# Cross-entropy of 8192 rows: a masked sum instead of gathers, a fixed order with shrinking last loads, and a strip of 16 small DMAs

## The chip, the cores and the metric

One core of one Trainium2 chip. The metric is device time in microseconds (us), lower is better; a verdict needs 2%. All runs told here were in the fast state at a granted clock of 1.0. Runs of one kernel agree within about 0.9 us, and the kernel before, run again beside the others in four sets of rounds, has medians of 2440.05 to 2440.22 us; so I read differences of 1 us here, although they are only 0.04% of the time. The 95% intervals are about ±0.14% or 3.4 us: by them alone, differences under about 3 us are not clear. The profile's span is about 1.7 us shorter than the time.

## The reference

```python
logits = np.random.randn(16, 512, 32000).astype(np.float32)      # 1048.6 MB
labels = np.random.randint(0, 32000, (16, 512)).astype(np.int32)

logits_max = np.max(logits, axis=-1, keepdims=True)
log_sum_exp = np.log(np.sum(np.exp(logits - logits_max), axis=-1)) + logits_max.squeeze(-1)
loss = -(logits - log_sum_exp[..., np.newaxis])[rows, cols, labels]
```

The 8192 rows lie as 64 groups of 128 rows, one row in each partition. Each logit is read once. The kernels leave the maximum out, as these inputs allow.

## The kernel before

Two buffers of 128x16000 take turns; ScalarE does Exp in place with a row sum. The last three groups come in loads of 4000 columns. The label's logit of each row is fetched by one indirect DMA per group ("gather" below) out of the logits in memory.

```python
    for g in range(G):                          # 64 gathers of 128 elements
        nc.gpsimd.indirect_dma_start(out=lab_logit[:, g:g + 1], ..., in_=lg,
            in_offset=bass.IndirectOffsetOnAxis(ap=idx[:, g:g + 1], axis=1))
    ...
            for c in range(C):                  # C = 2 halves of 16000 columns
                t = data_pool.tile([P, W], FP32)            # bufs=2
                nc.sync.dma_start(out=t[:], in_=lg_pg[:, g, c * W:(c + 1) * W])
                nc.scalar.activation(out=t[:], in_=t[:], func=Exp,
                                     accum_out=stats_col(g, c))
    ...                                         # last 3 groups: the same with 4000 columns, bufs=5
    finalize(0, G - 1)                          # sum, Ln, subtract, store
    finalize(G - 1, G)
```

The softmax here doesn't subtract the row's maximum and nothing guards it: scores larger than these inputs give would overflow.

Of the kernel before, what the change touches and what calls it, by code (L numbers as in the profile page):

```python
# [1 line left out]

# [4 lines left out]

FP32 = mybir.dt.float32
I32 = mybir.dt.int32  # L10


@with_exitstack
def kernel(
    ctx: ExitStack,
    tc: tile.TileContext,
    logits: bass.AP,
    labels: bass.AP,
    out: bass.AP,
):  # L20
    nc = tc.nc

    B, S, V = logits.shape
    N = B * S
    P = 128
    G = N // P
    assert N % P == 0

    W = 16000
    C = V // W  # L30
    assert V % W == 0

    WF = 4000
    CF = V // WF
    FINE_GROUPS = 3
    assert V % WF == 0

    lg = logits.rearrange("b s v -> (b s) v")
    lg_pg = lg.rearrange("(p g) v -> p g v", g=G)
    labels_pg = labels.rearrange("b s -> (b s)").rearrange("(p g) -> p g", g=G)  # L40
    out_pg = out.rearrange("b s -> (b s)").rearrange("(p g) -> p g", g=G)

    data_pool = ctx.enter_context(tc.tile_pool(name="data", bufs=2))
    fine_pool = ctx.enter_context(tc.tile_pool(name="fine", bufs=5))
    persist = ctx.enter_context(tc.tile_pool(name="persist", bufs=1))

    labs64 = persist.tile([P, G], mybir.dt.int64)
    nc.sync.dma_start(out=labs64[:], in_=labels_pg)  # L48

    idx = persist.tile([P, G], I32)  # L50
    nc.gpsimd.iota(idx[:], pattern=[[V, G]], base=0, channel_multiplier=G * V)  # L51
    labs32 = labs64[:].bitcast(I32).rearrange("p (g two) -> p g two", two=2)[:, :, 0]
    nc.gpsimd.tensor_tensor(out=idx[:], in0=idx[:], in1=labs32, op=mybir.AluOpType.add)  # L53

    lab_logit = persist.tile([P, G], FP32)
    for g in range(G):
        nc.gpsimd.indirect_dma_start(  # L57
            out=lab_logit[:, g:g + 1],
            out_offset=None,
            in_=lg,  # L60
            in_offset=bass.IndirectOffsetOnAxis(ap=idx[:, g:g + 1], axis=1),
        )

    stats = persist.tile([P, G - 1, CF], FP32)
    stats_last = persist.tile([P, 1, CF], FP32)
    nc.vector.memset(stats[:], 0.0)  # L66

    def stats_col(g, c):
        return stats[:, g, c:c + 1] if g < G - 1 else stats_last[:, 0, c:c + 1]

    for g in range(G):
        if g >= G - FINE_GROUPS:
            for c in range(CF):
                tf = fine_pool.tile([P, WF], FP32)
                nc.sync.dma_start(out=tf[:], in_=lg_pg[:, g, c * WF:(c + 1) * WF])
                nc.scalar.activation(  # L76
                    out=tf[:], in_=tf[:],
                    func=mybir.ActivationFunctionType.Exp,
                    accum_out=stats_col(g, c),
                )  # L80
        else:
            for c in range(C):
                t = data_pool.tile([P, W], FP32)
                nc.sync.dma_start(out=t[:], in_=lg_pg[:, g, c * W:(c + 1) * W])  # L84
                nc.scalar.activation(  # L85
                    out=t[:], in_=t[:],
                    func=mybir.ActivationFunctionType.Exp,
                    accum_out=stats_col(g, c),
                )

    totals = persist.tile([P, G], FP32)
    logsum = persist.tile([P, G], FP32)
    res = persist.tile([P, G], FP32)

    def finalize(lo, hi):
        nc.vector.reduce_sum(  # L96
            out=totals[:, lo:hi],
            in_=stats[:, lo:hi, :] if hi <= G - 1 else stats_last[:],
            axis=mybir.AxisListType.X,
        )  # L100
        nc.scalar.activation(  # L101
            out=logsum[:, lo:hi], in_=totals[:, lo:hi],
            func=mybir.ActivationFunctionType.Ln,
        )
        nc.vector.tensor_tensor(  # L105
            out=res[:, lo:hi], in0=logsum[:, lo:hi], in1=lab_logit[:, lo:hi],
            op=mybir.AluOpType.subtract,
        )
        nc.scalar.dma_start(out=out_pg[:, lo:hi], in_=res[:, lo:hi])  # L109

    finalize(0, G - 1)
    finalize(G - 1, G)


# [1 line left out]
_INS = ['logits', 'labels']  # L116
_OUTS = [((16, 512), 'float32')]


# [23 lines left out]
```

## Time and profile before

| | before |
|---|---|
| time, median | 2440.22 us (2440.01 to 2440.32) |
| read from memory | 1048.67 MB, 430 GB/s over the span |
| ScalarE / VectorE busy | 72% / 0% |
| steady distance of big loads | 18.90 us (8.192 MB, so 433 GB/s) |
| from the last landing to the end of the span | 7.9 us |

ScalarE waits for every big load (642.9 us idle), so the loads set the pace. The timeline of ScalarE in the middle (start, duration, what, idle before and cause):

```profile
349.45 13.54 ACT L85 ACTIVATE t<-t 128x16000 f32<-128x16000 f32 x1 [5.28 <-DMA t<-in_logits_dram]
...
368.35 13.54 ACT L85 ACTIVATE t<-t 128x16000 f32<-128x16000 f32 x1 [5.26 <-DMA t<-in_logits_dram]
...
387.25 13.54 ACT L85 ACTIVATE t<-t 128x16000 f32<-128x16000 f32 x1 [5.28 <-DMA t<-in_logits_dram]
```

An activation that waited for its load starts about 0.5 us after the last row of that load has ended (0.54 us in the median of the 122 big loads, from the packets of this trace), so these starts are a clock of landings: one every 18.90 us. The same timeline at the end:

```profile
2430.84 3.54 ACT L76 ACTIVATE tf<-tf 128x4000 f32<-128x4000 f32 x1 [1.11 <-DMA tf<-in_logits_dram]
...
2434.49 1.28 ACT L101 ACT_TABLE_LOAD   x1
...
2435.78 0.20 ACT L101 ACTIVATE logsum<-totals 128x1 f32<-128x1 f32 x1
2436.02 0.16 DVE L105 TENSOR_TENSOR res<-logsum,lab_logit 128x1 f32<-128x1 f32 x1 [1.35 <-ACT logsum L101]
```

The last tile landed at 2430.8; Exp, a table load, Ln, the subtraction and the store follow, 7.9 us in all.

### The profile page before, as it was taken

What the parts mean: (1) busy time and instruction counts of PE and PEld (TensorE: products, weight loads), DVE (VectorE), ACT (ScalarE), POOL (GpSimd) and SP (SyncE); (2) the same over time, 40 slices, a digit from 0 to 9 for tenths busy, and PEclk for the clock granted to TensorE, in tenths of its full rate; (3) what the DMA queues carried; (4) which work ended last, traced back from release to release, by engine and by line L of the source; (5) the groups of instructions that cost most, each with busy time, mean ns of one, the idle gap of its engine ahead of it and who ended that gap; (6) DMA issues with size and microseconds to landing.
All of it is one profiled execution on the core that took longest, in us unless ns stands there. A gap on an engine that the chain in (4) does not pass through costs nothing.

```text
span 2438.7 us, 851 instructions
## 1 busy us (share of the span) xinstructions
DVE 1.7 (0%) x5; ACT 1754.4 (72%) x298; POOL 61.2 (3%) x70
## 2 busy tenths in 40 slices
DVE  0000000000000000000000000000000000000000
ACT  4777766777677767777677767777677767777697
POOL 3222000000000000000000000000000000000000
DMA  9999999999999999999999999999999999999998
GB/s 404 437 420 422 435 437 435 429 429 437 437 436 428 431 435 437 435 432 428 435 436 436 435 427 434 436 437 435 427 432 436 437 435 425 434 437 432 426 430 360
DMA packets 23510, 1048.77 MB, mean 430 GB/s; under 512 B 4688, under 2 KB 4816, under 8 KB 4816
## 3 DMA queue, kind: packets, MB, share of 16 engines
q1 hardware_dynamic: 21168, 1048.65, 99.6%
q0 software_dynamic: 2048, 0.04, 0.1%
q10 hardware_dynamic: 288, 0.03, 0.0%
q14 instruction: 6, 0.05, 0.0%
HBM read 1048.67 MB, written 0.03 MB: 430 GB/s over the span
## 4 chain that ended last, share of the span: by engine, by line
DMA 63%; ACT 36%; issue 0%; ACTq 0%; SPq 0%; DVE 0%
DMA t<-in_logits_dram 61%; ACT t L85 34%; DMA tf<-in_logits_dram 2%; ACT tf L76 2%; ACT L101 0%; ACT L76 0%; ACTq L85 0%; ACT logsum L101 0%; SPq L84 0%; DVE res L105 0%; SPq L48 0%; ACTq L109 0%; ACTq L76 0%
## 5 line engine op out<-in xcount | busy, mean ns | idle before, releaser
L85 ACT ACTIVATE t<-t 128x16000 f32<-128x16000 f32 x122 | 1651.4, 13536 | 642.9 <-DMA t<-in_logits_dram 642.9
L76 ACT ACTIVATE tf<-tf 128x4000 f32<-128x4000 f32 x24 | 84.7, 3530 | 14.6 <-DMA tf<-in_logits_dram 14.6
L57 POOL DMA_INDIRECT lab_logit<-in_logits_dram,idx x64 | 60.5, 945 | 186.8 <-DMA lab_logit<-in_logits_dram,idx 184.2
L85 ACT ACTIVATION_READ_ACCUMULATOR t<-t 128x1 f32 x122 | 22.7, 186 | 0.0
L85 ACT ACT_TABLE_LOAD x1 | 1.3, 1283 | 23.3 <-DMA t<-in_logits_dram 23.3
L76 ACT ACTIVATION_READ_ACCUMULATOR tf<-tf 128x1 f32 x24 | 4.5, 187 | 0.0
L101 ACT ACT_TABLE_LOAD x2 | 2.6, 1283 | 0.0
L96 DVE TENSOR_REDUCE totals<-stats 128x63 f32<-128x504 f32 x1 | 0.7, 678 | 2394.9 <-ACT tf L76 2394.9
L76 ACT ACT_TABLE_LOAD x1 | 1.3, 1283 | 0.8 <-DVE res L105 0.8
L66 DVE MEMSET stats<- 128x504 f32 x1 | 0.5, 478 | 0.9 <-PEq L127 0.9
L101 ACT ACTIVATE logsum<-totals 128x63 f32<-128x63 f32 (+1 forms) x2 | 0.5, 229 | 0.0
L105 DVE TENSOR_TENSOR res<-logsum,lab_logit 128x63 f32<-128x63 f32 (+1 forms) x2 | 0.4, 192 | 2.2 <-ACT logsum L101 2.2
L53 POOL TENSOR_TENSOR idx<-idx,labs 128x64 int32<-128x64 int32 x1 | 0.3, 318 | 1.8 <-DMA labs<-in_labels_dram 1.8
L96 DVE TENSOR_REDUCE totals<-stats_last 128x1 f32<-128x8 f32 x1 | 0.2, 161 | 36.4 <-ACT tf L76 36.4
L51 POOL IOTA idx<- 128x64 int32 x1 | 0.2, 172 | 0.4 <-PEq L138 0.4
L127 POOL MEMSET const-uint8-127<- 128x1 uint8 x1 | 0.1, 118 | 0.0
L127 POOL MEMSET const-bfloat16-1.0<- 128x1 bf16 x1 | 0.1, 113 | 0.0
L127 POOL MEMSET const-float32-0.0<- 128x1 f32 x1 | 0.1, 98 | 0.2 <-issue 0.2
L127 POOL MEMSET const-float32-1.0<- 128x1 f32 x1 | 0.1, 104 | 0.0
## 6 DMA issues: line engine op xcount, KB each, us to landing
t<-in_logits_dram SPq DMA_DIRECT2D x122, 8000.0 KB, 24.1
tf<-in_logits_dram SPq DMA_DIRECT2D x24, 2000.0 KB, 20.1
lab_logit<-in_logits_dram,idx POOLq DMA_INDIRECT x64, 33.4
labs<-in_labels_dram SPq DMA_DIRECT2D x1, 64.0 KB, 1.9
out_dram<-res ACTq DMA_DIRECT2D x1, 31.5 KB, 9.1
out_dram<-res ACTq DMA_DIRECT2D x1, 0.5 KB, 1.4
```

The costliest lines, as they stand in the source:

```text
L51: nc.gpsimd.iota(idx[:], pattern=[[V, G]], base=0, channel_multiplier=G * V)
L53: nc.gpsimd.tensor_tensor(out=idx[:], in0=idx[:], in1=labs32, op=mybir.AluOpType.add)
L57: nc.gpsimd.indirect_dma_start(out=lab_logit[:, g:g + 1], out_offset=None, in_=lg, in_offset=bass.IndirectOffsetOnAxis(ap=idx[:, g:g + 1], ...
L66: nc.vector.memset(stats[:], 0.0)
L76: nc.scalar.activation(out=tf[:], in_=tf[:], func=mybir.ActivationFunctionType.Exp, accum_out=stats_col(g, c),)
L85: nc.scalar.activation(out=t[:], in_=t[:], func=mybir.ActivationFunctionType.Exp, accum_out=stats_col(g, c),)
L96: nc.vector.reduce_sum(out=totals[:, lo:hi], in_=stats[:, lo:hi, :] if hi <= G - 1 else stats_last[:], axis=mybir.AxisListType.X,)
L101: nc.scalar.activation(out=logsum[:, lo:hi], in_=totals[:, lo:hi], func=mybir.ActivationFunctionType.Ln,)
L105: nc.vector.tensor_tensor(out=res[:, lo:hi], in0=logsum[:, lo:hi], in1=lab_logit[:, lo:hi], op=mybir.AluOpType.subtract,)
L127: nc = _bacc.Bacc("TRN2", target_bir_lowering=False, num_devices=1)
```

## The change

It wants more of the DMA and a shorter end. 62 of the 64 gathers are replaced by VectorE, which compares column numbers with the label and sums the one logit that matches, in four operations of 4000 columns per tile. Exp then works in place, behind VectorE, in two halves. A third buffer is added, instructions keep the order in which they are written, the last loads shrink from 7400 to 960 columns so that the last Exp is short, and Exp and Ln share one table set. One strip of 960 columns is loaded by 16 DMAs of 15, 14, ... 1 and 8 rows, meant to set the 16 DMA engines apart in time (the "stagger" below).

```diff
+    plan(
+        G - 1,
+        [[7400, 5840, 2260], [4540, 3720, 2920, 1780, 1460, 1120], [960]], ...
+    data = ctx.enter_context(tc.tile_pool(name="data", bufs=3))
+    masked = psum.tile([P, H], FP32)                      # H = 4000, GG = G - 2
...
+    ctx.enter_context(tc.manual_schedule())
+    nc.scalar.dma_start(out=labs64[:], in_=labels_pg)
+    nc.scalar.preload_act_table_set("natural_log_exp_and_others")
-    for g in range(G):
+    for g in range(GG, G):
         nc.gpsimd.indirect_dma_start(...)
...
+        if (g, c0) == (1, 0):
+            p0 = 0
+            for k in list(range(15, 0, -1)) + [8]:
+                nc.sync.dma_start(
+                    out=t[p0:p0 + k, at:at + SKEW], in_=lg_pg[p0:p0 + k, g, c0:c0 + SKEW]
+                )
+                p0 += k
+            nc.sync.dma_start(out=t[:, at + SKEW:at + n], in_=lg_pg[:, g, c0 + SKEW:c0 + n])
+        else:
+            nc.sync.dma_start(out=t[:, at:at + n], in_=lg_pg[:, g, c0:c0 + n])
+        if g < GG:
+            for i in range(n // H):
...
+                nc.vector.scalar_tensor_tensor(
+                    out=masked[:], in0=cols[:], scalar=lab_at[:, h, g:g + 1],
+                    in1=t[:, lo:lo + H], op0=ALU.is_equal, op1=ALU.mult,
+                    accum_out=found[:, g, h:h + 1],
+                )
+                if n == W and i % 2 == 1:
+                    exp(g, t[:, lo - H:lo + H])
...
```

More of the change, by code (lines that the diff above doesn't have):

```diff
@@ L7 @@
 from concourse._compat import with_exitstack
+from concourse.masks import make_identity
 FP32 = mybir.dt.float32
 I32 = mybir.dt.int32
+EXP = mybir.ActivationFunctionType.Exp
+LN = mybir.ActivationFunctionType.Ln
+ALU = mybir.AluOpType
+X = mybir.AxisListType.X
 @with_exitstack
@@ L23 @@
     B, S, V = logits.shape
-    N = B * S
     P = 128
-    G = N // P
-    assert N % P == 0
+    G = B * S // P
     W = 16000
-    C = V // W
-    assert V % W == 0
-    WF = 4000
-    CF = V // WF
-    FINE_GROUPS = 3
-    assert V % WF == 0
+    H = 4000
+    NH = V // H
+    SKEW = 960
     lg = logits.rearrange("b s v -> (b s) v")
@@ L41, with plan @@
     out_pg = out.rearrange("b s -> (b s)").rearrange("(p g) -> p g", g=G)
-    data_pool = ctx.enter_context(tc.tile_pool(name="data", bufs=2))
-    fine_pool = ctx.enter_context(tc.tile_pool(name="fine", bufs=5))
+    GG = G - 2
+    loads = []
+    def plan(g, widths_by_buffer, order):
+        n_buffers = 1 + max((l[1] for l in loads), default=-1)
+        for b, i in order:
+            ws = widths_by_buffer[b]
+            loads.append((g, n_buffers + b, sum(ws[:i]), ws[i]))
+    plan(0, [[4000, 4000, 8000], [16000]], [(0, 0), (0, 1), (0, 2), (1, 0)])
@@ L45 @@
+    for g in range(1, G - 2):
+        plan(g, [[W], [W]], [(0, 0), (1, 0)])
+    plan(G - 2, [[W], [10000, 6000]], [(0, 0), (1, 0), (1, 1)])
+    plan(
+        G - 1,
+        [[7400, 5840, 2260], [4540, 3720, 2920, 1780, 1460, 1120], [960]],
+        [(0, 0), (0, 1), (1, 0), (1, 1), (1, 2), (0, 2), (1, 3), (1, 4), (1, 5), (2, 0)],
+    )
+    assert sum(l[3] for l in loads) == G * V
+    data = ctx.enter_context(tc.tile_pool(name="data", bufs=3))
     persist = ctx.enter_context(tc.tile_pool(name="persist", bufs=1))
+    psum = ctx.enter_context(tc.tile_pool(name="psum", bufs=1, space=bass.MemoryType.PSUM))
@@ L47 @@
+    masked = psum.tile([P, H], FP32)
     labs64 = persist.tile([P, G], mybir.dt.int64)
-    nc.sync.dma_start(out=labs64[:], in_=labels_pg)
-    idx = persist.tile([P, G], I32)
-    nc.gpsimd.iota(idx[:], pattern=[[V, G]], base=0, channel_multiplier=G * V)
     labs32 = labs64[:].bitcast(I32).rearrange("p (g two) -> p g two", two=2)[:, :, 0]
-    nc.gpsimd.tensor_tensor(out=idx[:], in0=idx[:], in1=labs32, op=mybir.AluOpType.add)
+    cols = persist.tile([P, H], mybir.dt.uint16)
+    idx = persist.tile([P, G - GG], I32)
@@ L55 @@
+    lab_at = persist.tile([P, NH, G], FP32)
+    found = persist.tile([P, GG, NH], FP32)
     lab_logit = persist.tile([P, G], FP32)
-    for g in range(G):
+    K = 10
+    sums = persist.tile([P, G - 1, 5], FP32)
+    sums_last = persist.tile([P, K], FP32)
+    totals = persist.tile([P, G - 1], FP32)
+    logsum = persist.tile([P, G - 1], FP32)
+    res = persist.tile([P, G - 1], FP32)
+    part = persist.tile([P, 1], FP32)
+    logsum_last = persist.tile([P, 1], FP32)
+    res_last = persist.tile([P, 1], FP32)
@@ L57 @@
+    ctx.enter_context(tc.manual_schedule())
+    nc.scalar.dma_start(out=labs64[:], in_=labels_pg)
+    nc.scalar.preload_act_table_set("natural_log_exp_and_others")
+    nc.vector.memset(sums[:], 0.0)
+    nc.gpsimd.iota(cols[:], pattern=[[1, H]], base=0, channel_multiplier=0)
+    nc.gpsimd.iota(idx[:], pattern=[[V, G - GG]], base=GG * V, channel_multiplier=G * V)
+    nc.gpsimd.tensor_tensor(out=idx[:], in0=idx[:], in1=labs32[:, GG:G], op=ALU.add)
+    for g in range(GG, G):
         nc.gpsimd.indirect_dma_start(
@@ L60 @@
             in_=lg,
-            in_offset=bass.IndirectOffsetOnAxis(ap=idx[:, g:g + 1], axis=1),
+            in_offset=bass.IndirectOffsetOnAxis(ap=idx[:, g - GG:g - GG + 1], axis=1),
         )
-    stats = persist.tile([P, G - 1, CF], FP32)
-    stats_last = persist.tile([P, 1, CF], FP32)
-    nc.vector.memset(stats[:], 0.0)
-    def stats_col(g, c):
-        return stats[:, g, c:c + 1] if g < G - 1 else stats_last[:, 0, c:c + 1]
-    for g in range(G):
-        if g >= G - FINE_GROUPS:
-            for c in range(CF):
-                tf = fine_pool.tile([P, WF], FP32)
-                nc.sync.dma_start(out=tf[:], in_=lg_pg[:, g, c * WF:(c + 1) * WF])
-                nc.scalar.activation(
-                    out=tf[:], in_=tf[:],
-                    func=mybir.ActivationFunctionType.Exp,
-                    accum_out=stats_col(g, c),
-                )
-        else:
-            for c in range(C):
-                t = data_pool.tile([P, W], FP32)
-                nc.sync.dma_start(out=t[:], in_=lg_pg[:, g, c * W:(c + 1) * W])
-                nc.scalar.activation(
-                    out=t[:], in_=t[:],
-                    func=mybir.ActivationFunctionType.Exp,
-                    accum_out=stats_col(g, c),
-                )
@@ L91 @@
-    totals = persist.tile([P, G], FP32)
-    logsum = persist.tile([P, G], FP32)
-    res = persist.tile([P, G], FP32)
-    def finalize(lo, hi):
-        nc.vector.reduce_sum(
-            out=totals[:, lo:hi],
-            in_=stats[:, lo:hi, :] if hi <= G - 1 else stats_last[:],
-            axis=mybir.AxisListType.X,
-        )
-        nc.scalar.activation(
-            out=logsum[:, lo:hi], in_=totals[:, lo:hi],
-            func=mybir.ActivationFunctionType.Ln,
-        )
-        nc.vector.tensor_tensor(
-            out=res[:, lo:hi], in0=logsum[:, lo:hi], in1=lab_logit[:, lo:hi],
-            op=mybir.AluOpType.subtract,
-        )
-        nc.scalar.dma_start(out=out_pg[:, lo:hi], in_=res[:, lo:hi])
@@ L111, with exp @@
-    finalize(0, G - 1)
-    finalize(G - 1, G)
+    for h in range(NH):
+        nc.vector.tensor_scalar(
+            out=lab_at[:, h, :], in0=labs32, scalar1=float(-h * H), scalar2=None, op0=ALU.add
+        )
+    buffers = {}
+    col = {}
+    n_exp = {}
+    def exp(g, ap):
+        k = n_exp.get(g, 0)
+        n_exp[g] = k + 1
+        s = sums[:, g, k:k + 1] if g < G - 1 else sums_last[:, k:k + 1]
+        nc.scalar.activation(out=ap, in_=ap, func=EXP, accum_out=s)
+    for j, (g, b, at, n) in enumerate(loads):
+        if b not in buffers:
+            buffers[b] = data.tile([P, W], FP32, tag="t", name="t")
+        t = buffers[b]
+        c0 = col.get(g, 0)
+        col[g] = c0 + n
+        if (g, c0) == (1, 0):
[3 more added lines that the diff above has]
+                    out=t[p0:p0 + k, at:at + SKEW], in_=lg_pg[p0:p0 + k, g, c0:c0 + SKEW]
+                )
+                p0 += k
+            assert p0 == P
+            nc.sync.dma_start(out=t[:, at + SKEW:at + n], in_=lg_pg[:, g, c0 + SKEW:c0 + n])
+        else:
+            nc.sync.dma_start(out=t[:, at:at + n], in_=lg_pg[:, g, c0:c0 + n])
+        if g < GG:
+            for i in range(n // H):
+                h = c0 // H + i
+                lo = at + i * H
+                nc.vector.scalar_tensor_tensor(
+                    out=masked[:],
+                    in0=cols[:],
+                    scalar=lab_at[:, h, g:g + 1],
+                    in1=t[:, lo:lo + H],
+                    op0=ALU.is_equal,
+                    op1=ALU.mult,
+                    accum_out=found[:, g, h:h + 1],
+                )
+                if n == W and i % 2 == 1:
+                    exp(g, t[:, lo - H:lo + H])
+            if n < W:
+                exp(g, t[:, at:at + n])
+        else:
+            exp(g, t[:, at:at + n])
+        left = len(loads) - 1 - j
+        if left == 6:
+            nc.vector.reduce_sum(out=totals[:], in_=sums[:], axis=X)
+            nc.vector.reduce_sum(out=lab_logit[:, 0:GG], in_=found[:], axis=X)
+        if left == 4:
+            nc.scalar.activation(out=logsum[:], in_=totals[:], func=LN)
+            nc.vector.tensor_tensor(out=res[:], in0=logsum[:], in1=lab_logit[:, 0:G - 1], op=ALU.subtract)
+        if left == 1:
+            nc.vector.reduce_sum(out=part[:], in_=sums_last[:, 0:K - 1], axis=X)
@@ L116 @@
+    assert n_exp[G - 1] == K
+    nc.sync.dma_start(out=out_pg[:, 0:G - 1], in_=res[:])
+    nc.scalar.activation(out=logsum_last[:], in_=sums_last[:, K - 1:K], func=LN, bias=part[:])
+    nc.vector.tensor_tensor(out=res_last[:], in0=logsum_last[:], in1=lab_logit[:, G - 1:G], op=ALU.subtract)
+    nc.sync.dma_start(out=out_pg[:, G - 1:G], in_=res_last[:])
 _INS = ['logits', 'labels']
```

## The prediction

> **What bounds it now.** The stream of loads. The page gives DMA 90% busy or more in every slice but the last, 1048.67 MB read, 430 GB/s over the span; ScalarE 72%, VectorE 0%. In the timeline of ScalarE the big activations start every 18.90 us from about 270 us on (8.192 MB at 433 GB/s), the 4000-column ones every 4.76: together about 0.05 us fixed per load and 434.5 GB/s. ScalarE needs 13.5 us of each 18.90. So saved compute doesn't count; only loads that start sooner, run without gaps, or end closer to the finish.
>
> The span (2438.7 us): first load starts at 1.65; about 2420 us of loads at the steady rate; about 9 us lost; last tile landed at 2430.8; then 7.9 us (Exp 3.54, table load 1.28, Ln 0.20, subtract 0.16, store). Lost, from the single DMA packets: about 3.2 us in the first 260 us, where rows take 2.37 to 2.43 instead of 2.36 us while 64 indirect gathers run; 0.7 us at the first row; 0.7 us at the third load (issued after the first activation, which sat behind a table load).
>
> **What the change does.**
> - 62 of 64 gathers go: −3.1 us of DMA.
> - Third buffer, small first loads: the late third load goes, −0.7. The labels move to another queue: first load 0.45 sooner.
> - 139 large loads instead of 146: −0.2.
> - Strip: [...] But engines are 0.9 to 2.2 us apart already, with rows at 2.361 to 2.369 us, so I expect nothing back in the steady rate[...].
> - Masked sum: 496 VectorE operations of 4000 fp32. [...] Under 18.90, so off the path in the middle.
> - But ScalarE now follows VectorE: a tile's last Exp ends about 24.6 us after landing instead of 13.5. After the last masked tile ScalarE has 64000 columns (0.833 ns each, 0.19 us an operation: 56.5 us) while the loads take 76.1: 24.6 + 56.5 = 81.1, about 4.5 us (rounded down) after the last landing. The shrinking widths don't reach their 1 us.
> - One table set for Exp and Ln: −1.28 in the tail; from the last Exp's end 3.1 us instead of 4.3.
> - Tail altogether 7.5 instead of 7.9.
>
> **Sum.** −0.45 −3.1 −0.7 −0.2 +0.5 −0.4 ≈ −4.4 us: predicted time 2436 us, 2431 to 2439.5. Faster by over 2%: 0.01 (the bytes forbid it); within: 0.93; slower: 0.06.
>
> **What would show it.** VectorE about 90% busy, 4.3 to 4.5 us per operation; 18.90 us tile period already before 260 us; no 3 us row at the third load; last landing near 2427; ScalarE without idle time in the last 30 us, its last Exp ending 4 to 5 us after the last landing.
>
> **What would make it wrong.** VectorE over 4.72 us per operation (it then sets the pace[...]); the strip's 17 issues starving the queue; the stagger speeding up every row (to 2361 ns: −3 us); a faster VectorE, so less lag at the end (up to −3.5).

The sum came to −4.4 us, so 2436 us; its +0.5 is the strip, and its −0.4 rests on the 24.6 us of ScalarE behind the landing. The runs give these numbers afterwards: 4.39 us an operation and 4.49 from one to the next, and the last Exp of the last masked tile 24.8 us after its landing (2360.9 to 2385.7 us). The 0.833 ns a column is what the page of before gives, (13536 − 3530) ns over 12000 columns, and the 0.19 us its 186 ns for reading the accumulator; the last rows of one load on the 16 engines end 0.5 to 2.6 us apart in that trace.

## More of the kernel before

The page of the kernel before: busy times, rates in 40 slices, the DMA queues, then groups with count, busy us, mean ns, idle time before them and its cause.

```profile
span 2438.7 us, 851 instructions
...
DVE 1.7 (0%) x5; ACT 1754.4 (72%) x298; POOL 61.2 (3%) x70
...
GB/s 404 437 420 422 435 437 435 429 429 437 437 436 428 431 435 437 435 432 428 435 436 436 435 427 434 436 437 435 427 432 436 437 435 425 434 437 432 426 430 360
...
q14 instruction: 6, 0.05, 0.0%
...
L85 ACT ACTIVATE t<-t 128x16000 f32<-128x16000 f32 x122 | 1651.4, 13536 | 642.9 <-DMA t<-in_logits_dram 642.9
...
L57 POOL DMA_INDIRECT lab_logit<-in_logits_dram,idx x64 | 60.5, 945 | 186.8 <-DMA lab_logit<-in_logits_dram,idx 184.2
```

## The result, and the profile after

The changed kernel took 2446.21 us (2446.09 to 2446.47, 4 runs) beside 2440.22: **6 us slower**, outside the predicted range. The ratio is 1.0025, with a 95% interval of 1.0011 to 1.0039. A ratio here is the mean time of one kernel's fast runs over that of the other's of the same rounds, so it is not quite the ratio of the quoted medians. The page after:

```profile
span 2444.7 us, 2141 instructions
...
DVE 2211.1 (90%) x1006; ACT 1784.5 (73%) x527; POOL 13.3 (1%) x9
...
GB/s 387 435 435 434 434 428 431 436 436 436 434 434 431 429 434 435 435 436 436 433 430 428 435 436 435 436 436 431 429 432 435 436 435 435 435 432 430 431 432 311
...
q14 instruction: 16, 0.13, 0.0%
...
L146 DVE SCALAR_TENSOR_TENSOR masked<-cols,lab_at,t 128x4000 f32<-128x4000 uint16 x496 | 2179.4, 4394 | 161.2 <-DMA t<-in_logits_dram 148.2
```

VectorE costs what was predicted: 4.39 us an operation, started every 4.49, and 90% busy. The first slice fell from 404 to 387 GB/s and the last from 360 to 311; the packets of instruction loads rose from 6 to 16. VectorE now gives the clock of landings; its timeline at the start:

```profile
22.63 4.39 DVE L146 SCALAR_TENSOR_TENSOR masked<-cols,lab_at,t 128x4000 f32<-128x4000 uint16 x1 [4.45 <-DMA t<-in_logits_dram]
...
42.14 4.39 DVE L146 SCALAR_TENSOR_TENSOR masked<-cols,lab_at,t 128x4000 f32<-128x4000 uint16 x1 [10.57 <-DMA t<-in_logits_dram]
...
65.78 4.39 DVE L146 SCALAR_TENSOR_TENSOR masked<-cols,lab_at,t 128x4000 f32<-128x4000 uint16 x1 [5.72 <-DMA t<-in_logits_dram]
```

The third tile, the one with the strip, landed 23.64 us after the second instead of 18.90. What the queue that issues loads waited for, in total us, times and longest, and then the DMA in short stretches (the last two columns are the DMA share and GB/s):

```profile
SPq L134 <- DMA t<-in_logits_dram: 32.4, 3, 19.2
```

```profile
38.00:40.00 2.00, 0.00 (x0) 0.57 (x2) 0.00 (x0) 1.00 1.18 512
40.00:42.00 2.00, 0.00 (x0) 0.00 (x0) 0.00 (x0) 1.00 0.56 140
42.00:44.00 2.00, 1.86 (x1) 0.00 (x0) 0.00 (x0) 1.00 0.26 65
44.00:46.00 2.00, 2.00 (x1) 0.00 (x0) 0.00 (x0) 1.00 0.72 221
```

Line 134 issues the strip. It had to wait three times for earlier loads to land, 32.4 us in all, and towards the end of these waits the engines ran dry: 140, 65, 221 GB/s. (A packet is counted where it starts, hence 512. Why the issues had to wait, the trace does not show.) Later in the run:

```profile
387.54 4.39 DVE L146 SCALAR_TENSOR_TENSOR masked<-cols,lab_at,t 128x4000 f32<-128x4000 uint16 x1 [0.98 <-DMA t<-in_logits_dram]
...
407.42 4.39 DVE L146 SCALAR_TENSOR_TENSOR masked<-cols,lab_at,t 128x4000 f32<-128x4000 uint16 x1 [1.96 <-DMA t<-in_logits_dram]
...
426.31 4.39 DVE L146 SCALAR_TENSOR_TENSOR masked<-cols,lab_at,t 128x4000 f32<-128x4000 uint16 x1 [0.98 <-DMA t<-in_logits_dram]
```

18.89, but once 19.88: a landing 0.98 us late. This comes back at 673 and 939 us and so on, about every 265 us.

The single packets of the trace, which no view lists, show why. A row here is the packet of 64000 bytes that fills one partition; each of the 16 engines carries 8 of a load's 128 (followed through the kernel before, each carries 976 of the 15616 rows of its 122 big loads). About 16 us before each late landing, within the same load, one 8192-byte packet of the queue "instruction" runs for 0.31 to 0.33 us, which I read as the fetch of a block of instructions (127 of them, see below). The next row on one DMA engine starts that much later, and itself takes 3.02 us where rows take 2.366 on average: 0.32 + 0.66 = 0.98 us. Why the row itself is longer stays open. Packets carry no engine number, but an engine's row starts within about 0.1 us of the end of its last one, so engines can be followed; as far as they can be, all these fetches fall on the same engine.

The trace lists 1143 instructions of VectorE with its waits, and 9 such fetches: one for 127 instructions. Fetches name no owner either; that these are VectorE's is inferred from their number and spacing, and tested below. Five more, which by their number go with ScalarE's 669 instructions, fall on another engine and cost it about 0.7 us each (the row behind takes 2.74 us).

Every big load has rows on all 16 engines, and what waits for it starts after the last of them (the 0.54 us of the kernel before are counted from the last of all 128 rows), so the delays of that one engine add up. At the end it finished 2436.5 us into the span, alone: 13 of the others had finished 8.5 to 9.4 us earlier. (Before, the slowest was 0.6 to 2.0 us behind the others.) That is the 311 GB/s of the last slice.

VectorE itself shows no stop for its fetches: in the list of what it waited for, no wait stands without a known cause ("issue"). The loads do: 0.98 us on one DMA engine for each.

The end of ScalarE's timeline, which answers to that of before:

```profile
2378.86 6.87 ACT L121 ACTIVATE t<-t 128x8000 f32<-128x8000 f32 x1 [1.96 <-DVE masked L146]
...
2385.73 13.52 ACT L121 ACTIVATE t<-t 128x16000 f32<-128x16000 f32 x1
...
2440.63 0.99 ACT L121 ACTIVATE t<-t 128x960 f32<-128x960 f32 x1
...
2441.74 0.29 ACT L174 ACTIVATE logsum_last<-sums_last,part 128x1 f32<-128x1 f32 x1
```

ScalarE has no idle time after 2378.86, when the last masked tile was released to it. The last data row ended at 2436.5, so by the 0.5 us between row end and Exp that the kernel before shows, it landed at 2437.0 (an estimate), and the last Exp ended at 2441.6, 4.6 us later. That part had been predicted.

### The profile page after: what moved, and what is told of

Same layout as the page of the kernel before. It is cut to its first block, busy times and chain, and to the rows that moved or that the text cites. A ratio compares the mean times of both kernels' runs of the same rounds, so it can differ in the third digit from the quotient of the medians.

```text
span 2444.7 us, 2141 instructions
## 1 busy us (share of the span) xinstructions
DVE 2211.1 (90%) x1006; ACT 1784.5 (73%) x527; POOL 13.3 (1%) x9
## 2 busy tenths in 40 slices
DMA packets 20784, 1048.82 MB, mean 429 GB/s; under 512 B 2720, under 2 KB 2848, under 8 KB 3488
## 4 chain that ended last, share of the span: by engine, by line
DMA 81%; DVE 15%; ACT 2%; issue 1%; SPq 0%; DVEq 0%
DMA t<-in_logits_dram 81%; DVE masked L146 15%; ACT t L121 2%; SPq L134 0%; DVEq L146 0%; SPq L141 0%; SPq L139 0%; ACT logsum_last L174 0%; DVE res_last L175 0%; ACT logsum L167 0%
## 5 line engine op out<-in xcount | busy, mean ns | idle before, releaser
L146 DVE SCALAR_TENSOR_TENSOR masked<-cols,lab_at,t 128x4000 f32<-128x4000 uint16 x496 | 2179.4, 4394 | 161.2 <-DMA t<-in_logits_dram 148.2
L121 ACT ACTIVATE t<-t 128x8000 f32<-128x8000 f32 (+4 forms) x262 | 1759.7, 6716 | 656.3 <-issue 372.9
L146 DVE DVE_READ_ACCUMULATOR masked<-cols,lab_at,t 128x1 f32 x496 | 70.6, 142 | 0.0
L121 ACT ACTIVATION_READ_ACCUMULATOR t<-t 128x1 f32 x262 | 48.8, 186 | 0.0
L101 POOL DMA_INDIRECT lab_logit<-in_logits_dram,idx x2 | 9.3, 4653 | 0.9 <-POOL idx L99 0.5
```

Source lines behind the costliest of these rows:

```text
L101: nc.gpsimd.indirect_dma_start(out=lab_logit[:, g:g + 1], out_offset=None, in_=lg, in_offset=bass.IndirectOffsetOnAxis(ap=idx[:, g - GG:g ...
L121: nc.scalar.activation(out=ap, in_=ap, func=EXP, accum_out=s)
L146: nc.vector.scalar_tensor_tensor(out=masked[:], in0=cols[:], scalar=lab_at[:, h, g:g + 1], in1=t[:, lo:lo + H], op0=ALU.is_equal, op1=ALU. ...
```

## The experiments

The theory after the first look has four parts: the strip runs the engines dry (+4.7 us), VectorE's instruction fetches delay one DMA engine (about 9 x 0.98 us), ScalarE's lag behind VectorE eats the shorter end (3.5 us), and the rest of the change gains as predicted. The rivals: the stagger helps and pays; VectorE's traffic with the data, not its instructions, disturbs the loads; the lag hides behind the late engine. All kernels are correct unless said otherwise.

### No strip (e1_no_strip)

```diff
-        if (g, c0) == (1, 0):
+        if False:
```

> The changed kernel with the strip taken out: the first half of the second group is one 128x16000 load again. Theory (the strip runs the DMA engines dry): in the trace of the changed kernel the third tile landed 23.64 us after the second instead of 18.90, so 4.7 us go away[...]: 2440.5 to 2441.5 us. Rival (the stagger itself helps the later rows and pays for part of the gap): less than 3 us go away, or rows get longer than 2365 ns on average. In either case the once-per-265-us late landings (+0.98 us) of the changed kernel stay.

Measured: 2441.37 us (before in the same rounds 2440.10), 4.84 less than the changed kernel. The first tiles now land regularly; the second pair of lines is of the late landing:

```profile
41.72 4.39 DVE L146 SCALAR_TENSOR_TENSOR masked<-cols,lab_at,t 128x4000 f32<-128x4000 uint16 x1 [10.04 <-DMA t<-in_logits_dram]
...
60.61 4.39 DVE L146 SCALAR_TENSOR_TENSOR masked<-cols,lab_at,t 128x4000 f32<-128x4000 uint16 x1 [0.98 <-DMA t<-in_logits_dram]
...
382.41 4.39 DVE L146 SCALAR_TENSOR_TENSOR masked<-cols,lab_at,t 128x4000 f32<-128x4000 uint16 x1 [0.98 <-DMA t<-in_logits_dram]
...
402.28 4.39 DVE L146 SCALAR_TENSOR_TENSOR masked<-cols,lab_at,t 128x4000 f32<-128x4000 uint16 x1 [1.96 <-DMA t<-in_logits_dram]
```

The first pair is 18.89 us apart. The late landings every 265 us stayed (19.87 from 382 to 402 us). Rows take 2.366 us on average with the strip and without it. So the strip costs 4.8 us and gives nothing back. It could not have left the stagger that it was meant for: the engines ran dry, and all but one took up their next row within 0.72 us of each other.

### The same strip in 3 DMAs (e2_strip3)

```diff
-            for k in list(range(15, 0, -1)) + [8]:
+            for k in [64, 32, 32]:
```

> The changed kernel with the same 960-column strip loaded by 3 DMAs (64, 32, 32 partitions[...]) instead of 16. Theory: the cost is the number of issues, since the issuing queue waited for earlier loads to land before it could issue more (32.4 us in 3 waits), not the narrow rows: time as without the strip plus at most 0.5 us, and the third tile lands 18.9 to 19.4 us after the second. Rival: rows of 3840 bytes are slow in themselves: at least 2 us remain.

Measured: 2442.89 us, 1.5 more than without the strip, 3.3 less than with 16 DMAs. This lies between the two expectations. Around the strip the issuing queue waited only for the labels here (3.9 us) and issued the rest of the tile some 34 us before its first row, so about two thirds of the cost are put down to the 16 issues. (How the rows of either strip fall on the engines was not shown, nor what part of the 3.3 us that is.) The last third is in the packets: rows of 3840 bytes took 0.15 us at first and then up to 0.3, and the first wide rows behind them 2.4 to 2.9 instead of 2.22. Why is left open; it is not the width alone, for the last 960-column load takes 0.15 a row.

### The kernel before, with useless VectorE copies (e3_before_dve9)

```diff
+                for i in range(9):
+                    nc.vector.tensor_copy(out=scratch[:, i:i + 1], in_=stats_col(g, c))
```

> The kernel before, with 9 useless one-column VectorE copies after each big Exp (about 1100 VectorE instructions in all[...]; nobody waits for them). Theory (each 8192-byte fetch of a VectorE's instructions stops one and the same DMA engine for about 0.97 us, and all loads wait for the slowest engine): 8 or 9 fetches on one engine, that engine 7.8 to 8.7 us behind at the end instead of the 2 us of the kernel before: 2445.5 to 2447 us, and big landings that come 0.98 us late every 120 to 130 instructions' worth of time. Rival (the changed kernel is slow because of what VectorE does with the data, or because of the strip): 2440 to 2441 us.

Measured: 2448.45 us, 8.35 more than the kernel before in the same rounds, for copies of one column (145 ns each on the page) that nobody waits for. The expectation was 2445.5 to 2447. The page has 16 instruction packets where the kernel before has 6:

```profile
DVE 79.5 (3%) x1103; ACT 1754.4 (72%) x298; POOL 61.2 (3%) x70
...
q14 instruction: 16, 0.13, 0.0%
```

ScalarE's timeline, to be held against the lines of before from 349 us on:

```profile
349.81 13.54 ACT L87 ACTIVATE t<-t 128x16000 f32<-128x16000 f32 x1 [5.26 <-DMA t<-in_logits_dram]
...
369.73 13.54 ACT L87 ACTIVATE t<-t 128x16000 f32<-128x16000 f32 x1 [6.29 <-DMA t<-in_logits_dram]
...
388.58 13.54 ACT L87 ACTIVATE t<-t 128x16000 f32<-128x16000 f32 x1 [5.22 <-DMA t<-in_logits_dram]
```

19.92 where 18.90 stood: a landing about 1 us late, which comes ten times in the run. I had counted 1100 instructions; with its waits VectorE has 1235, so ten fetches, not nine (one for about 123 instructions): 10 x 0.98 = 9.8, less about 1.6 us that three late landings had cost before (0.3, 0.7 and 0.7 us at 406, 1220 and 2033 us), gives 8.2. This settles the second part: the instructions alone do it, with next to no data behind them.

### The kernel before, with 2 gathers (e4_before_2gathers)

```diff
-    for g in range(G):
+    nc.vector.memset(lab_logit[:], 0.0)
+    for g in range(G - 2, G):
         nc.gpsimd.indirect_dma_start(
```

> The kernel before, with only the last 2 of the 64 gathers (the result is wrong on purpose: the other label logits are zero). Both theories: the gathers cost DMA time in the first 260 us, about 3.2 us: 2437 us, with rows of 2.36 to 2.37 us from the second tile on. If the early loss is start-up of the engines and not the gathers: 2439.5 to 2440.5.

The result is wrong. Measured: 2435.48 us, 4.6 less than the kernel before, so 0.074 us for each of the 62 gathers left out. I had expected 3.2: the sum of the longer rows, averaged over engines, had been lessened by what I put down to start-up. The run also has one instruction packet less (5 on the page); what that is worth was not tested apart. Landings give the cost directly: from the third to the fifteenth tile 230.5 us before, 226.8 here.

### The last 4 groups gathered (e5_last4_gathered)

```diff
-    GG = G - 2
+    GG = G - 4                                            # and no strip
```

> The changed kernel without the strip, and with the last 4 groups' label logits gathered instead of the last 2, so that the last 4 loads before the shrinking ones wait for no VectorE. Theory (in the kernel without the strip ScalarE was 24.9 us behind the landing after the last masked tile and had no idle time from there on, which put its last Exp 4 to 5 us after the last landing): the lag is worked off, the last Exp ends about 1 us after the last landing, ScalarE has idle time before its last Exps: 3.5 us less than 2441.4, and up to 1 us less if there is one VectorE fetch less: 2437 to 2438. Rival (the end is set by the late DMA engine alone, ScalarE's lag is hidden behind it): 2440.5 to 2441.5.

Measured: 2437.86 us, 3.5 less than without the strip alone. The page still has 16 instruction packets, and the last row ends at the same time as there (2431.5 against 2431.4 us into the span), so the gain is not in the loads. ScalarE at the end:

```profile
2402.56 6.37 ACT L121 ACTIVATE t<-t 128x7400 f32<-128x7400 f32 x1 [0.46 <-DMA t<-in_logits_dram]
...
2432.02 1.00 ACT L121 ACTIVATE t<-t 128x960 f32<-128x960 f32 x1
```

It waits for the loads again, and the last Exp starts 0.5 us after the last row ended (2431.5). The shrinking widths reach their aim once the lag is gone; the last part of the prediction's reasoning holds.

### All gathers (e6_all_gathers)

```diff
-    GG = G - 2
+    GG = 0                                                # no masked sum, and no strip
...
-    masked = psum.tile([P, H], FP32)
```

> The changed kernel without the strip and without the masked sum: all 64 gathers as in the kernel before, but three buffers, fixed order, one table set and the shrinking last loads. Theory: the VectorE fetches (about 9 of 0.97 us on one engine) are gone, the slowest engine is again one with some 3 ScalarE fetches (2 us); the gathers cost 4.6 us as measured; the end is 4 us after the last landing instead of 7.9; the first load is 0.4 us sooner and the third 0.7: about 5 us less than the kernel before: 2434.5 to 2436. Rival (masked sum is the cheaper way, as I thought: gathers cost 4.6 us, VectorE nothing): 2442 or more.

Measured: 2435.67 us, 4.4 less than the kernel before. The page again has 6 instruction packets, and the slowest engine is 0.6 to 2.4 us behind the others instead of 8 or 9:

```profile
DVE 1.3 (0%) x5; ACT 1748.8 (72%) x281; POOL 61.2 (3%) x70
...
q14 instruction: 6, 0.05, 0.0%
```

So the replacement that was the heart of the change is a loss: 60 gathers cost 4.4 us on every engine (60 x 0.074; in the kernel before, rows on each of the 16 took 2.40 to 2.41 us in the first 260 us and 2.366 later), the nine fetches of the masked sum 8.8 us on one, of which some 2 us were slack that the engine with ScalarE's fetches leaves anyway, since all loads wait for it too (8.8 − 2 − 4.4 = 2.4 us of loss, an estimate; measured 2.2 from here to the kernel with the last 4 gathered).

### A stagger without running dry (e7_spare_stagger)

```diff
+        if 0 <= j - 43 < 15:
+            k = 15 - (j - 43)
+            nc.sync.dma_start(out=spare[0:k, :], in_=lg_pg[0:k, g, 0:SKEW])   # no strip
```

> The changed kernel without the strip, with 15 small loads of 15 to 1 rows of 3840 bytes into a tile that nobody reads, one behind each of 15 big loads around 400 to 700 us, so that they queue behind data and no engine runs dry. [...] Theory (a stagger gives nothing back): rows stay at 2365 ns on average; the time is that of the kernel without the strip plus 0.15 us for each small row that falls on the engine that is behind anyway: 2441.3 to 2443.7[...]. Rival (stagger speeds the rows up): under 2440.5, rows nearer to 2361 ns after 700 us.

Measured: 2446.32 us, 5 more than without the strip, outside both expectations. About 0.5 us of it was there before the first small load (the landing at 762 us). (The rows of the small loads lie at 796 to 1070 us, not at 400 to 700: I had misreckoned the distance of the loads.) Landings behind the first six came 0.3 to 0.7 us late, and the rows next to each small load took up to 3.0 us, at first on all 16 engines, also on those that had no small row (15 rows or fewer can't give one to each of the 16). From 1075 to 2000 us rows took 2366 ns on average, as without the strip, so no gain of the stagger shows. Why a small load slows rows of engines that have no part in it stays open; the issuing queue is not the cause, as the next big load was issued about 9 us before its first row. With this a test of the pure stagger failed: what is shown is that small DMAs between big ones cost about 0.3 us each here, not what a stagger without them would do.

### 20 groups masked (e8_mask20), and 9 (e9_mask9)

```diff
-    GG = G - 2
+    GG = 20                                               # e9: GG = 9; no strip in both
```

> The changed kernel without the strip, only the first 20 groups masked on VectorE, the other 44 gathered. Theory: 2 or 3 VectorE fetches (2 to 2.9 us on their engine, little more than the ScalarE's 2 us on another), 44 gathers at 0.074 us (3.3 us), no lag of ScalarE at the end: 1.0 to 1.5 us less than with all gathers: 2433.5 to 2435. Rival (the cost of the masked sum does not go with its fetches, but with its data): between the all-gathers kernel and the all-masked kernel in proportion, 20/62 of their difference above the former.

Measured: 2435.66 us: no gain over all gathers, a miss of both expectations. 13 of the 16 engines did finish earlier than there (2.7 to 3.6 us before the slowest, against 1.3 to 2.4 for most), as 20 gathers less would have it, but three VectorE fetches (the page has 9 instruction packets, not 6) put one engine further behind. A masked group costs 0.14 us on one engine (nine fetches for 62 groups), a gathered one 0.074 on all; only the slack that the engine with ScalarE's fetches gives anyway, about 2 us, is free.

> As the kernel with the first 20 groups masked, but only the first 9. Theory: VectorE fetches once or twice (1 to 2 us on their engine, below or level with the 2 us of the engine with the ScalarE's fetches), so the slowest engine is no later than with all gathers, while 9 gathers less save 0.074 us each (0.7 us): 2434.6 to 2435.4, a little under both the kernel with all gathers (2435.67) and the one with 20 groups masked (2435.66). If it is 2435.6 or more, the balance of gathers against fetches is not what sets these three times.

Measured: 2435.10 us (2434.94 to 2435.22), ratio to before 0.998 (0.9966 to 0.9993). With one or two fetches (8 packets on the page) the free slack is used and no more. It is the fastest version found, 5.0 us under the kernel before and 11.1 under the changed one; its lead over all gathers, 0.57 us from other rounds, is small, though no run of the one overlaps with one of the other. Its end:

```profile
2429.06 1.00 ACT L121 ACTIVATE t<-t 128x960 f32<-128x960 f32 x1
...
2430.19 0.29 ACT L174 ACTIVATE logsum_last<-sums_last,part 128x1 f32<-128x1 f32 x1
```

### The sum

The kernels form a chain from before to after, in medians, which come from different rounds; the first step was not split further:

| step | from | to | us |
|---|---|---|---|
| third buffer, order, one table set, shrinking loads | before 2440.1 | all gathers 2435.67 | −4.4 |
| masked sum for 60 groups instead of gathers | 2435.67 | last 4 gathered 2437.86 | +2.2 |
| masked sum up to the last loads (ScalarE's lag) | 2437.86 | no strip 2441.37 | +3.5 |
| strip of 16 DMAs | 2441.37 | after 2446.21 | +4.8 |
| all | | | +6.1 |

## Why the prediction was wrong

- **Bound by the stream of loads, no large gain possible:** right.
- **The strip, +0.5 in the sum:** the term that was mis-sized, 4.8 us instead of 0.5. I counted its bytes and an imbalance of the engines (my estimate: no run here shows it), and not that its issues would wait for earlier loads to land, 32.4 us in 3 waits. "The strip's 17 issues starving the queue" stood only among what could go wrong. 3.3 us of it went with the 16 issues, 1.5 stayed with the narrow rows in 3 DMAs.
- **The masked sum, "under 18.90, so off the path in the middle":** this step failed. VectorE is off the path, with 4.39 us an operation and 4.49 from one to the next, inside the 4.3 to 4.5 predicted. But its instructions are not: 9 fetches of 0.98 us on one DMA engine that all loads wait for. The sum had no term for them. They show in the late landings, the packets, and in the kernel before with copies that do nothing (+8.35 us). With the strip this covers the gap: the predicted last landing was 2427, the estimate for the measured one is 2437. As an estimate in the sum's own terms: +4.3 (strip, 4.8 less 0.5), +6.8 (fetches, 8.8 less the 2 of slack), −1.5 (gathers, 4.6 instead of 3.1) make 9.6 of the 10.2 us between 2436 and 2446.2.
- **Gathers, −3.1 us:** right in kind, too small: 4.6.
- **Third load and first load:** the first row started 0.5 us sooner (1.75 against 2.27), as predicted. Without the strip the third tile landed 18.89 us after the second instead of 19.66, also as predicted; in the changed kernel the strip brought the slow first rows back there (2.7 to 3.2 us).
- **ScalarE's lag at the end:** right in mechanism and size. Predicted 4.5 us after the last landing, measured 4.6; taking it away gave 3.5 us.
- **Tail 7.5 instead of 7.9:** measured about 7.7 (2444.7 less the estimated landing at 2437.0).
- **The stagger gives nothing back in the steady rate:** no gain was seen, but the strip never set the stagger in a steady stream, and the attempt to set it cost time of its own. Not settled.

## What to carry to other kernels

In a kernel that only streams, count instructions even on an engine that seems free: here fetching them was DMA traffic (16 packets, 0.13 MB of 1048.82), it fell on one DMA engine for VectorE (0.98 us each) and on another for ScalarE (about 0.7), and each load waited for the slowest, 8.5 to 9.4 us behind 13 of the others at the end. Work off the path must also not become the gate of the engine that ends the kernel; gate it early, not in the last tiles (3.5 us here). And small DMAs in a stream of big ones can leave the DMA engines without work, as 16 of them did here (down to 65 GB/s, 4.8 us in all), so look at what the issuing queue waits for, not at the bytes.
